# Prompt attention by pairs of heads: values and probabilities as two float32r parts in place of one float32 product

## Chip, cores and metric

One core of a Trainium2 chip. The metric is the device time of one execution in microseconds (us): a run's time is what counts, and the profile of one execution tells where it went. Engines are called as in the profile: PE (TensorE matmul), PEld (its weight load), DVE (VectorE), ACT (ScalarE), POOL (GpSimd), SP (SyncE, which issues the transfers).

## What is computed

Two decoder layers, for a prompt of 512 tokens and for 8 x 8 decode tokens. Each layer has a retention branch, an attention branch over the keys that an indexer selects, gates, and projections. The part around the change is the attention of the prompt, for 8 query heads that share 2 key/value heads (4 to 1) of 64 channels:

```
att = jnp.einsum('btkgd,btjkd->btkgj', qg, kg) * (ATT_HEAD_DIM ** -0.5)
att = jnp.where(valid[:, :, None, None, :], att, -jnp.inf)
p = jax.nn.softmax(att, axis=-1)
o = jnp.einsum('btkgj,btjkd->btkgd', p, vg)
```

The kernel doesn't gather: it scores all causal keys of a block of 128 queries, adds a large negative bias where the indexer left a key out, and takes the softmax over what is left.

## The kernel before

Everything is float32 in the reference. The kernel multiplies most of it as float32r (one pass through the array, fewer bits of the operands) in two parts: a matrix is split into a high part and the rest (`split`, `convert`), and products high x high, low x high and high x low are summed in PSUM. Activations are `xh`/`xl` (or `oh`/`ol`), weights `whi`/`wlo`; the big projections are `pm<-xh,whi`, `pm<-xl,whi`, `pm<-xh,wlo` with 288 or 256 columns. A few products are plain float32; the trace shows each of these as two records.

The tokens are five blocks: j = 0 to 3 are 128 prompt tokens each, j = 4 the 64 decode tokens. Per layer, in the order of `PLAN`: keys and values (`kx`), indexer (`iq`), retention values (`rv`), the attention gate (`az`), queries (`aq`, u = 0 and 1, four heads each), retention's q, k and gate for four heads (`rt0` to `rt3`), two of the eight gates of each branch (`gr`, `ga`), and from there on the merge (`wo`), which needs every branch to be done.

**Who sets the order.** All of this is written as generators (`head`, `kx`, `ret_p`, `ret_s`, `attend_s`, ...), the side streams, beside one main stream of projections. `Streams.go` emits instructions one by one: of all streams' next operations it takes the one that could start first by a model of the engines (`_duration`, `HOP`, `MARGIN`), and at equal starts the one of smaller `PRIO`. What is emitted is each engine's program order, and the engines run it in that order. All instructions are emitted in one line (293), so rows of the trace are told apart by tile names. The tiles `raw[0]`, `raw[1]` lie over the buffers `xh`, `xl` and carry those names.

For POOL the model charges the same for whatever operation (n is the number of elements of a partition):

```
    if eng == "POOL":
        return 0.3 + 0.165 * n
```

In before POOL only does powers of a few columns (`rsqrt`).

**Prompt attention** (`attend`, lines 925 to 944, and `head`, 898 to 921). For block j: 8 heads, at most `HEADS_IN_FLIGHT` = 3 at once. One head is a chain over four engines: scores (two matmuls into the one PSUM bank `tq`), the biased minimum on DVE (`CUSTOM_DVE`), exp with its sum on ACT, a reciprocal on DVE, the scaling on ACT, j + 1 transposes on PE into the one bank `ta`, a copy to SBUF on ACT (`t2k<-ta`), and j + 1 float32 products with 64 columns of values as stationary operand, into the one bank `oT`:

```
            for k in range(j + 1):
                yield PE.matmul(oT[kv * 64:(kv + 1) * 64, g * 128:(g + 1) * 128], av[:, k, kv * 64:(kv + 1) * 64],
                                PT[:, k * 128:(k + 1) * 128], start=k == 0, stop=k == j)
```

After all 8 heads of a block (`yield done`) DVE multiplies `oT` with the gate (`silz`), and the next block begins. The queries of a block, `qst[j, u]`, lie in one of 5 slots `QS`; probabilities and other intermediate tiles in 5 slots `T2` (`t2k`). The decode tokens have a stream of their own (`attend_s`, two groups g), which uses the same banks `tq`, `ta`, `oT`. So does the indexer with `tq`.

**The merge** waits for all side streams of the layer before it emits its splits `oh`/`ol` and the products with `wo` (line 1254):

```
                    for e in sides:
                        yield e
```

Of the kernel before, what the change touches and what calls it, by code (L numbers as in the profile page):

```python
# [11 lines left out]
FT = mybir.dt.float32  # L12
FR = mybir.dt.float32r
BF = mybir.dt.bfloat16
I32 = mybir.dt.int32
AF = mybir.ActivationFunctionType
OP = mybir.AluOpType
# [6 lines left out]
NS = 64  # L24
# [168 lines left out]


class Streams:
    """Emits the instructions of many sequential streams in the order in which a model of the engines could
    start them, so that each engine's program order follows what is ready."""

    HOP = {("DVE", "DVE"): 0.13, ("ACT", "ACT"): 0.13, ("POOL", "POOL"): 0.1, ("PE", "PE"): 0.0, ("SP", "SP"): 0.0,
           ("ACT", "PE"): 0.23, ("DVE", "PE"): 0.21, ("PE", "DVE"): 0.2, ("PE", "ACT"): 0.2, ("POOL", "DVE"): 0.07,  # L200
# [104 lines left out]
def tile_hybrid_decoder(ctx: ExitStack, tc: tile.TileContext, A, O):  # L305
    nc = tc.nc
    ctx.enter_context(tc.manual_schedule())
    K = Streams()
# [9 lines left out]
    def slots(pool, name, shape, dtype, n):  # L318
        return Slots([pool.tile(shape, dtype, name=f"{name}{i}") for i in range(n)])

    BANK = {n: slots(pb, n, [128, 512], FT, c) for n, c in BANKS.items()}
# [14 lines left out]
    def r3(ap, a):  # L336
        return ap.rearrange("p (a b) -> p a b", a=a)
# [51 lines left out]
    ready, paged = Event(), Event()  # L389
    second, third = Event(), Event()  # L390

    # ---- weights: one ordered sequence of units, each split into two float32r parts as it lands
    W = {}

    class Unit:
# [161 lines left out]
    def layer(l, xh, xl, kxb):  # L557
# [29 lines left out]
        at = atc.__enter__()  # L587
        raw = [xp.tile([128, KT * TX], FT, name="xh"), xp.tile([128, KT * T], FT, name="xl")]
        ro = 2 * (2 * T + 32)
        av = r3(raw[1][:, ro + 1152:ro + 1792], 5)  # L590
        iqss = raw[1][:, ro + 1792:ro + 2048].rearrange("p (b h t) -> p b h t", b=8, h=4)
        scs = [None] + [raw[1][:, ro + o:ro + o + (j + 2) * 128] for j, o in enumerate((0, 256, 640))]
        vr = r3(raw[0][:, 0:2560], 5)
# [14 lines left out]
        SM = slots(at, "sm", [128, 16], FT, 6)  # L608
        IQS = slots(at, "iqs", [128, 4, 128], FR, 2)
        QS = slots(at, "qs", [128, 4, 128], FR, NSLOT["qs"])  # L610
        T2 = slots(at, "t2k", [128, 512], FT, NSLOT["t2"])
        S4 = slots(at, "s4", [128, 8, 128], FT, NSLOT["s4"])
        TB = slots(at, "tb", [128, TH], FT, 2)
        SO = slots(at, "so", [128, 128], FT, 2)
# [63 lines left out]
        def kx(j, ps):  # L678
            yield ready
            yield e_r  # L680
            src, n, z = yield from pull(j, ps, 320)
            r = rcol[:n, j:j + 1]
            kt2 = yield Get(T2)
            kkt = kt2[:, :192]
            kk = r3(kkt[:n], 3)
            yield S.activation(kkt[:n], src[:, 0:192], AF.Copy, scale=r)
            yield S.activation(av[:n, j], src[:, 192:320], AF.Copy, scale=r)
            pulled(j, ps, z)
            kv = kk[:, 1:3]
            sqt = yield Get(SQ)  # L690
            sq = r3(sqt[:n, 0:128], 2)
            yield V.tensor_tensor(sq, kv, kv, OP.mult)
            yield from headnorm(kv, sq, n, 2)
            K.put(SQ, sqt)
            yield V.tensor_tensor(kv, kv, bc(gqk[:n, l, 1:2], [n, 2, 64]), OP.mult)
            yield from rope(kk, j, n, 3)
            rows = slice(j * 128, j * 128 + n)
            kdt = yield Get(KD)
            b = yield Get(BANK["ta"])
            if j < 4:  # L700
                kd = kdt[:, :384].rearrange("p (a b c) -> p a b c", a=3, b=2)
                yield S.activation(kd, bc(kk[:, :, None, :], [128, 3, 2, 64]), AF.Copy)
                for i in range(3):
                    yield PE.transpose(b[:, i * 128:(i + 1) * 128], flat(kd[:, i]), ident)
                K.put(KD, kdt)
                yield from split(kdh[:, :, rows], kdl[:, :, rows], r3(b[:, :384], 3))
            else:
                yield V.memset(kdt[:NS, 64:128], 0.0)
                yield V.tensor_copy(kdt[:NS, 0:64], kk[:, 0])
                yield PE.transpose(b[:, 0:NS], kdt[:NS, 0:128], ident[:NS, :NS])  # L710
                yield PE.transpose(b[:, NS:2 * NS], flat(kv), ident[:NS, :NS])
                K.put(KD, kdt)
                yield S.activation(flat(kts), b[:, :2 * NS], AF.Copy)
            K.put(BANK["ta"], b)
            K.set(e_kt[j])
            yield SP.dma_start(O["ik"][l, rows], kk[:, 0])
            yield SP.dma_start(O["k"][l, rows], flat(kv))
            yield SP.dma_start(O["v"][l, rows], av[:n, j])
            K.put(T2, kt2)
            K.set(e_k)  # L720

# [173 lines left out]
            yield S.activation(P, P, AF.Copy, scale=s)  # L895
            K.put(SM, sm)

        def head(j, u, g, kv, oT, done):
            L = max(256, (j + 1) * 128)
            bias = con("cb") if j == 0 else scs[j]  # L900
            q = qst[j, u][:, (g % 2) * 2 + kv]
            P = yield Get(T2)
            b = yield Get(BANK["tq"])
            ps = b[:, :L]
            yield PE.matmul(ps, q, kdh[:, 1 + kv, :L], start=True, stop=False)
            yield PE.matmul(ps, q, kdl[:, 1 + kv, :L], start=False, stop=True)
            yield from softmax(ps, bias, P[:, :L], b)
            PT = yield Get(T2)
            pT = yield Get(BANK["ta"])
            W_ = (j + 1) * 128  # L910
            for k in range(j + 1):
                yield PE.transpose(pT[:, k * 128:(k + 1) * 128], P[:, k * 128:(k + 1) * 128], ident)
            K.put(T2, P)
            yield S.activation(PT[:, :W_], pT[:, :W_], AF.Copy)
            K.put(BANK["ta"], pT)
            for k in range(j + 1):
                yield PE.matmul(oT[kv * 64:(kv + 1) * 64, g * 128:(g + 1) * 128], av[:, k, kv * 64:(kv + 1) * 64],
                                PT[:, k * 128:(k + 1) * 128], start=k == 0, stop=k == j)
            K.put(T2, PT)
            K.put(HD, None)  # L920
            K.set(done)

        HD = Slots([None] * HEADS_IN_FLIGHT)

        def attend():
            yield e_k
            for j in range(4):
                if j:
                    yield e_sc[j]
                oT = yield Get(BANK["oT"])  # L930
                done = Event(8)
                for u in range(2):
                    yield e_q[j, u]
                    for g in (2 * u, 2 * u + 1):
                        for kv in range(2):
                            yield Get(HD)
                            K.spawn(head(j, u, g, kv, oT, done), PRIO["attend"])
                yield done
                for u in range(2):
                    K.put(QS, qst[j, u])  # L940
                yield e_az
                z = silz[1][:, :, j * 128:(j + 1) * 128]
                yield V.tensor_tensor(z, r3(oT, 4), z, OP.mult)
                K.put(BANK["oT"], oT)

        def attend_s():
            yield paged
# [2 lines left out]
            for g in range(2):  # L950
# [11 lines left out]
                for kv in range(2):  # L962
# [20 lines left out]
                    yield S.activation(PT[:NS, 256:384], pT[:NS, 256:384], AF.Copy)  # L983
                    K.put(BANK["ta"], pT)
                    o = oS[:, kv * 64:(kv + 1) * 64]
                    yield PE.matmul(o, PT[:NS, 256:384], av[:NS, 4, hb], start=True, stop=True)
                    for b4 in range(4):
                        for i in range(2):
                            yield PE.matmul(o[b4 * 32:(b4 + 1) * 32],
# [473 lines left out]


PLAN = _plan("kx iq rv0 rv1 az0 az1 az2 az3 aq0 aq1 rt0 rt1 rt2 rt3")
HEADS_IN_FLIGHT = 3
PRIO = dict(convert=0, load=1, tables=6, indexer=7, indexer_s=3, attend=3, attend_s=5, ret_p=6, ret_s=4)
NSLOT = dict(s4=3, qs=5, t2=5, hi=3, lo=3)


def _prepare(x_prompt, x_sample, cache_k, cache_v, cache_idx_k, state_ret, page_table, p_prompt, p_sample,
# [79 lines left out]
```

## Time and profile before

| | us |
|---|---|
| median of 3 runs (1131.34 to 1132.42) | 1132.09 |
| span of the profiled execution | 1130.3 |
| median less span: what lies around the span | 1.8 |
| PE busy in the span | 1116.5 (99%) |
| DVE busy | 725.6 (64%) |
| ACT busy | 512.5 (45%) |
| POOL busy | 45.7 (4%) |

The profiled execution has no other time of its own in the result than its span; the 1.8 us around it are taken from the median. The profile's page gives the busy time of each engine, their shares in 40 slices of the span, the chain of work that ended last, and the costliest groups of instructions. A row of a group has the engine, the operation, the tile written and the tiles read, the shapes, the count, the busy time of all and the mean duration of one. Matmuls are pipelined: one lasts 0.28 us in the trace while the next starts after 0.12, so a matmul's cost to PE is read from the starts of two that follow each other.

### The profile page before, as it was taken

Reading aid. Unit: us, or ns where it says so; the run is one execution under the profiler, and the core shown is the slowest. Engines: PE = TensorE matmul, PEld = TensorE weight load, DVE = VectorE, ACT = ScalarE, POOL = GpSimd, SP = SyncE. Lnnn points to the kernel's source line nnn. Section 1 sums busy time; section 2 is a strip of 40 time slices with the busy share of each in tenths; the row PEclk is TensorE's granted clock in tenths of the full one; section 3 lists DMA queues with packets and bytes.
Section 4 is the critical chain, followed back from the end, with each engine's and each line's share of the span. In section 5 each row is a group of like instructions: output and inputs, shape, how many; then the busy total and the mean of one; then the engine's idle time right before and its main releaser. Section 6 shows DMA issues by size and latency. Waiting matters only on the chain.

```text
span 1130.3 us, 21562 instructions
## 1 busy us (share of the span) xinstructions
PE 1116.5 (99%) x8586; PEld 1058.9 (94%) x8586; DVE 725.6 (64%) x1883; ACT 512.5 (45%) x1084; POOL 45.7 (4%) x52
## 2 busy tenths in 40 slices
PE   8999999999999999999999999999999999999998
PEld 7899988888899999999999999888889999999998
DVE  6799988876464444543658999888654553544343
ACT  6643566647443232324546336656563422222331
POOL 0100200000000000000010012000000000000000
PEclk9999999999999999999999999999999999999999
DMA  6442221322122222523336112222212222234231
GB/s 196 139 133 76 76 75 52 102 78 78 59 75 75 93 76 92 172 92 109 100 118 181 59 57 94 74 79 80 73 60 78 75 78 91 75 130 144 93 113 48
DMA packets 43895, 105.92 MB, mean 94 GB/s; under 512 B 6418, under 2 KB 18578, under 8 KB 43794
## 3 DMA queue, kind: packets, MB, share of 16 engines
q1 hardware_dynamic: 43794, 104.55, 27.4%
q8 instruction: 67, 1.10, 0.4%
q14 instruction: 34, 0.28, 0.1%
HBM read 93.61 MB, written 10.91 MB: 92 GB/s over the span
## 4 chain that ended last, share of the span: by engine, by line
PE 91%; DVE 4%; DMA 2%; ACT 2%; issue 1%; SPq 0%; POOL 0%; DVEq 0%; ACTq 0%; POOLq 0%
PE pm L293 72%; PE oT L293 5%; PE tq L293 4%; PE acc L293 3%; PE tr L293 3%; PE ta L293 3%; DVE wlo L293 1%; DMA wst<-in_wb 1%; ACT whi L293 1%; DVE misc L293 1%; DMA x<-in_xT 1%; DVE silz L293 0%; DMA wst<-in_wq 0%; DVE qs L293 0%; DVE ol L293 0%
## 5 line engine op out<-in xcount | busy, mean ns | idle before, releaser
L293 PE MATMUL pm<-xl,whi 128*128 128x288 f32 x1536 | 458.7, 299 | 0.0
L293 PE MATMUL pm<-xh,wlo 128*128 128x288 f32 x1536 | 458.4, 298 | 0.0
L293 PE MATMUL pm<-xh,whi 128*128 128x288 f32 x1536 | 458.0, 298 | 0.4 <-DVE misc L293 0.4
L293 PEld LDWEIGHTS pm<-xl,whi 128*128 128x128 f32 x1536 | 290.1, 189 | 3.2 <-issue 2.4
L293 PEld LDWEIGHTS pm<-xh,whi 128*128 128x128 f32 x1536 | 290.2, 189 | 2.9 <-issue 1.6
L293 PEld LDWEIGHTS pm<-xh,wlo 128*128 128x128 f32 x1536 | 289.9, 189 | 1.8 <-issue 1.4
L293 ACT ACTIVATE whi<-wst 128x1024 fp32r<-128x1024 f32 (+4 forms) x148 | 150.5, 1019 | 280.5 <-PE pm L293 207.7
L293 DVE TENSOR_TENSOR wlo<-wst,whi 128x1024 fp32r<-128x1024 f32 (+4 forms) x148 | 173.0, 1171 | 88.8 <-ACT whi L293 88.5
L293 PE MATMUL pm<-whi,xh 128*128 128x256 f32 (+2 forms) x416 | 117.2, 288 | 0.7 <-ACT xl L293 0.7
L293 PE MATMUL pm<-wlo,xh 128*128 128x256 f32 (+2 forms) x416 | 117.0, 289 | 0.0
L293 PE MATMUL pm<-whi,xl 128*128 128x256 f32 (+2 forms) x320 | 91.0, 284 | 0.0
L293 DVE TENSOR_TENSOR misc<-pm,R 128x288 f32<-128x288 f32 x64 | 29.2, 457 | 90.1 <-PE pm L293 88.7
L293 ACT ACTIVATE t2k<-t2k,sm 128x256 f32<-128x256 f32 (+3 forms) x136 | 75.6, 581 | 22.6 <-DVE sm L293 19.4
L293 PEld LDWEIGHTS pm<-whi,xh 128*128 128x128 f32 x416 | 78.7, 189 | 2.5 <-issue 1.2
L293 PEld LDWEIGHTS pm<-wlo,xh 128*128 128x128 f32 x416 | 78.7, 189 | 1.6 <-issue 1.1
L293 PE MATMUL pm<-oh,whi 128*128 128x288 f32 x240 | 71.0, 296 | 0.0
L293 PE MATMUL pm<-oh,wlo 128*128 128x288 f32 x240 | 70.9, 296 | 0.0
L293 PE MATMUL pm<-ol,whi 128*128 128x288 f32 x240 | 70.9, 295 | 0.0
L293 PEld LDWEIGHTS pm<-whi,xl 128*128 128x128 f32 x320 | 60.5, 189 | 0.1
L293 ACT ACTIVATE misc<-misc 128x288 f32<-128x288 f32 x64 | 27.9, 436 | 60.5 <-DVE misc L293 60.5
L293 DVE MAX8 sm<-xl 128x8 f32<-128x384 f32 (+2 forms) x96 | 52.3, 548 | 0.3
L293 DVE SCALAR_TENSOR_TENSOR misc<-misc,pm 128x288 f32<-128x288 f32 x60 | 26.8, 451 | 39.3 <-PE pm L293 39.3
(231 smaller groups left out, 1654.3 us busy)
## 6 DMA issues: line engine op xcount, KB each, us to landing
wst<-in_wa SPq DMA_DIRECT2D x96, 512.0 KB, 3.5
wst<-in_wb SPq DMA_DIRECT2D x16, 512.0 KB, 4.1
wst<-in_wo SPq DMA_DIRECT2D x16, 512.0 KB, 3.4
s<-in_ckv SPq DMA_DIRECT2D x32, 128.0 KB, 2.4
s<-in_s SPq DMA_DIRECT2D x8, 512.0 KB, 4.3
out_rss<-s SPq DMA_DIRECT2D x8, 512.0 KB, 2.6
x<-in_xT SPq DMA_DIRECT2D x8, 288.0 KB, 4.5
misc<-in_xT SPq DMA_DIRECT2D x8, 288.0 KB, 3.6
```

Of the source, the lines that this page charges most:

```text
L293: op.fn(*op.a, **op.k)
```

## The change

For the prompt, the values get a second form: `vhl[:, k]` (128 keys x 256 columns, float32r) holds for each key/value head its 64 columns in a high and a low part, as [high 0 | low 0 | low 1 | high 1]. It is written in `kx` by two copies on ACT and two subtractions on DVE a block.

`head` becomes `score` (to the end of the softmax) and `pair`, which takes the two heads of one u and one kv together. Their transposes go side by side into `ta`, for two blocks of keys at a time; ACT copies them as float32r (`pth`, high part), DVE writes the rest (`ptl`), each with one buffer. Each block of keys then takes two products of 256 columns with the full 128 x 128 array: stationary [high | low] values, moving `pth`, then `ptl`. So rows 0 to 63 of the result have one of the parts of the values and rows 64 to 127 the other; a new stream `collect` adds the two halves (a copy on ACT, an addition on DVE, for each kv) and multiplies with the gate on POOL.

`attend` now has one bank `oT` and one `done` for each (j, u): it spawns two pairs, waits for both, then goes on to the next u. `PAIRS_IN_FLIGHT` is 2, `QS` has 4 slots, `T2` four own slots and one in `raw[1]`. Scores, softmax, the number of transposes, the decode attention and the retention stay.

```diff
+        vhl = at.tile([128, 4, 256], FR, name="vhl")
...
-        T2 = slots(at, "t2k", [128, 512], FT, NSLOT["t2"])
+        PTH = slots(at, "pth", [128, 512], FR, NSLOT["pt"])
+        PTL = slots(at, "ptl", [128, 512], FR, NSLOT["pt"])
+        T2 = slots(at, "t2k", [128, 512], FT, NSLOT["t2"] - 1)
+        T2.free.append(raw[1][:, ro + 1280:ro + 1792])
...
+            if j < 4:
+                for i, (h, o) in enumerate(((0, 64), (192, 128))):
+                    vh = vhl[:, j, h:h + 64]
+                    yield S.activation(vh, v[:, i * 64:(i + 1) * 64], AF.Copy)
+                    yield V.tensor_tensor(vhl[:, j, o:o + 64], v[:, i * 64:(i + 1) * 64], vh.bitcast(FT), OP.subtract)
...
+        def pair(j, u, kv, oT, first, done):
+            Ps, evs = [], []
+            for i in range(2):
+                P = yield Get(T2)
+                ev = Event()
+                K.spawn(then(score(j, qst[j, u][:, i * 2 + kv], kv, P), ev), PRIO["attend"])
+                Ps.append(P)
+                evs.append(ev)
+            o = oT[:, kv * 256:(kv + 1) * 256]
+            for k0 in range(0, j + 1, 2):
+                ks = range(k0, min(k0 + 2, j + 1))
+                w = len(ks) * 256
+                pT = yield Get(BANK["ta"])
+                for i in range(2):
+                    yield evs[i]
+                    for k in ks:
+                        yield PE.transpose(pT[:, (k - k0) * 256 + i * 128:(k - k0) * 256 + (i + 1) * 128],
+                                           Ps[i][:, k * 128:(k + 1) * 128], ident)
...
+                hi = yield Get(PTH)
+                lo = yield Get(PTL)
+                yield S.activation(hi[:, :w], pT[:, :w], AF.Copy)
+                yield V.tensor_tensor(lo[:, :w], pT[:, :w], hi[:, :w].bitcast(FT), OP.subtract)
+                K.put(BANK["ta"], pT)
+                for k in ks:
+                    for x in (hi, lo):
+                        yield PE.matmul(o, vhl[:, k, kv * 128:(kv + 1) * 128], x[:, (k - k0) * 256:(k - k0 + 1) * 256],
+                                        start=not first, stop=k == j and x is lo, skip_group_check=True)
...
+        def collect(j, u, oT, done):
+            yield done
+            t = yield Get(T2)
+            o = t[:, :256]
+            for kv in range(2):
+                mine, other = slice(kv * 64, kv * 64 + 64), slice(64 - kv * 64, 128 - kv * 64)
+                c = slice(kv * 256, (kv + 1) * 256)
+                yield S.activation(o[mine], oT[other, c], AF.Copy)
+                yield V.tensor_tensor(o[mine], oT[mine, c], o[mine], OP.add)
+            K.put(BANK["oT"], oT)
+            yield e_az
+            z = silz[1][:, 2 * u:2 * u + 2, j * 128:(j + 1) * 128]
+            yield G.tensor_tensor(z, r3(o, 2), z, OP.mult)
+            K.put(T2, t)
...
                 for u in range(2):
                     yield e_q[j, u]
-                    for g in (2 * u, 2 * u + 1):
-                        for kv in range(2):
-                            yield Get(HD)
-                            K.spawn(head(j, u, g, kv, oT, done), PRIO["attend"])
-                yield done
+                    oT = yield Get(BANK["oT"])
+                    done, first = Event(2), []
+                    for kv in range(2):
+                        yield Get(HD)
+                        K.spawn(pair(j, u, kv, oT, first, done), PRIO["attend"])
+                    last.append(Event())
+                    K.spawn(then(collect(j, u, oT, done), last[-1]), PRIO["attend"])
+                    yield done
                     K.put(QS, qst[j, u])
...
-HEADS_IN_FLIGHT = 3
+PAIRS_IN_FLIGHT = 2
...
-NSLOT = dict(s4=3, qs=5, t2=5, hi=3, lo=3)
+NSLOT = dict(s4=3, qs=4, t2=5, pt=1, hi=3, lo=3)
```

Three places show how the order moves. First PE in the last prompt block (j = 3) of layer 0, before. `tq` rows are scores, `ta` rows transposes of the probabilities, `oT` rows the products with the values, `pm` rows projections of the main stream:

```order
L293 MATMUL oT_73<-t2k_382,xl 64x128 x4
L293 MATMUL tq_71<-kdh,qs_378 128x512
L293 MATMUL tq_71<-kdl,qs_378 128x512
L293 MATMUL ta_72<-cst,t2k_384 128x128 x4
L293 MATMUL pm_68<-xl,whi_90 128x288
L293 MATMUL pm_68<-xh,wlo_93 128x288
L293 MATMUL pm_68<-xh,whi_90 128x288
```

Six more projections follow before the next head's `oT` row; after the layer's last `oT` row 169 more stand before the merge. The same block now (`tr` rows are the retention's):

```order
L293 MATMUL tq_71<-kdh,qs_381 128x512
L293 MATMUL tq_71<-kdl,qs_381 128x512
L293 MATMUL tr_74<-xl 128x128
L293 MATMUL ta_72<-cst,t2k_384 128x128 x2
L293 MATMUL tr_74<-cst,xl 128x128 x4
L293 MATMUL oT_73<-pth_382,vhl 128x256
L293 MATMUL oT_73<-ptl_383,vhl 128x256
```

No projection stands in it any more: of layer 0's PE order, the last 247 matmuls ahead of the merge (numbers 1944 to 2190 of the program) hold the decode attention's second group, the blocks (2,1), (3,0), (3,1) and the last retention pieces, and not one `pm` row; 134 projections in a row stand right ahead of them. The end of it, with the first row of the merge:

```order
L293 MATMUL oT_73<-pth_382,vhl 128x256
L293 MATMUL oT_73<-ptl_383,vhl 128x256
L293 MATMUL tr_74<-cst,xh 128x128 x4
L293 MATMUL pm_68<-oh_3775,whi_89 128x288
```

Where 169 projections stood between the last product with the values and the merge, now there is none. Layer 1 has the same stretch (numbers 5958 to 6204). Two shorter ones without projections stand earlier in each layer: 112 matmuls with the decode attention's first group and block (1,1) (1536 to 1647 in layer 0), and 34 with the end of block (1,0) (1356 to 1389). ACT at the start of block (3,0), now (`t2k,sm<-t2k,sm` is an exp with its sum, `t2k<-t2k,sm` the scaling of a head's probabilities):

```order
L293 ACTIVATE t2k_386,sm_375<-t2k_386,sm_375 128x512
L293 ACTIVATE t2k_384,sm_371<-t2k_384,sm_371 128x512
L293 ACTIVATE t2k_386<-t2k_386,sm_375 128x512
L293 ACTIVATE t2k_385,sm_373<-t2k_385,sm_373 128x512
L293 ACTIVATE t2k_384<-t2k_384,sm_371 128x512
L293 ACTIVATE t2k_387,sm_374<-t2k_387,sm_374 128x512
```

Each head's scaling stands behind the next head's exp.

## Rows read from the trace of the kernel before

**Rows 1.** The page: busy us and shares; PE's granted clock in 40 slices.
```profile
PE 1116.5 (99%) x8586; PEld 1058.9 (94%) x8586; DVE 725.6 (64%) x1883; ACT 512.5 (45%) x1084; POOL 45.7 (4%) x52
...
PEclk9999999999999999999999999999999999999999
```

**Rows 2.** Stretches: length, busy us of PE, PEld, DVE, ACT, POOL, PEclk, DMA.
```profile
0.00:28.00 28.00, 22.45 (x140) 21.73 (x140) 17.29 (x29) 18.33 (x35) 0.28 (x5) 1.00 0.61 198
...
268.00:297.00 29.00, 29.00 (x212) 25.44 (x210) 13.13 (x44) 17.48 (x37) 1.01 (x1) 1.00 0.19 68
297.00:326.00 29.00, 29.00 (x239) 27.60 (x239) 15.24 (x40) 12.30 (x26) 1.70 (x2) 1.00 0.21 76
```

**Rows 3.** The page: chain that ended last, by engine.
```profile
PE 91%; DVE 4%; DMA 2%; ACT 2%; issue 1%; SPq 0%; POOL 0%; DVEq 0%; ACTq 0%; POOLq 0%
```

**Rows 4.** Timeline of PE around one float32 product (start, duration, then the instruction).
```profile
126.24 0.28 PE L293 MATMUL pm<-whi,xh 128*128 128x256 f32 x1
126.36 0.28 PE L293 MATMUL pm<-whi,xl 128*128 128x256 f32 x1
126.57 0.43 PE L293 MATMUL oT<-t2k,xl 128*64 128x128 f32 x2
126.94 0.39 PE L293 MATMUL pm<-wlo,xh 128*128 128x256 f32 x1
```

**Rows 5.** Timeline of PE around the layer's last four float32 products; the merge's first row.
```profile
295.23 0.29 PE L293 MATMUL pm<-xl,whi 128*128 128x288 f32 x1
295.46 1.09 PE L293 MATMUL oT<-t2k,xl 128*64 128x128 f32 x8
296.47 0.33 PE L293 MATMUL tr<-cst,xl 128*128 128x128 f32 x1
...
325.51 0.30 PE L293 MATMUL pm<-oh,whi 128*128 128x288 f32 x1
```

**Rows 6.** Timeline, block 3: scores to DVE; exp, sum and scaling on ACT.
```profile
271.29 0.47 PE L293 MATMUL tq<-kdh,qs 128*128 128x512 f32 x1
271.60 0.39 PE L293 MATMUL tq<-kdl,qs 128*128 128x512 f32 x1
272.14 0.69 DVE L293 CUSTOM_DVE_ANT_0 t2k<-tq,xl 128x512 f32<-128x512 f32 x1 [1.31 <-PE tq L293]
...
284.43 0.71 ACT L293 ACTIVATE t2k<-t2k,sm 128x512 f32<-128x512 f32 x1
...
285.46 0.72 ACT L293 ACTIVATE t2k<-t2k,sm 128x512 f32<-128x512 f32 x1 [0.23 <-DVE sm L293]
```

**Rows 7.** Timeline, block 3: four transposes and the copy behind them.
```profile
286.05 0.66 PE L293 MATMUL ta<-cst,t2k 128*128 128x128 f32 x4
...
286.74 0.60 ACT L293 ACTIVATE t2k<-ta 128x512 f32<-128x512 f32 x1 [0.56 <-PE ta L293]
```

**Rows 8.** DVE and ACT groups by shape: PSUM reads and the merge's splits.
```profile
L293 DVE TENSOR_TENSOR silz<-oT,silz 128x512 f32<-128x512 f32 x8 | 5.5, 687 | 1.1 <-PE oT L293 1.0
...
L293 DVE TENSOR_TENSOR qs<-ta,qs 64x256 fp32r<-64x256 f32 x32 | 13.5, 422 | 3.0 <-ACT qs L293 2.1
...
L293 ACT ACTIVATE qs<-ta 64x256 fp32r<-64x256 f32 x32 | 12.0, 376 | 11.4 <-PE ta L293 6.0 <-DVE qs L293 5.0
...
L293 ACT ACTIVATE xh<-acc,gs 128x128 f32<-128x128 f32 x48 | 18.9, 453 | 5.1 <-DVE gs L293 5.1
```

**Rows 9.** POOL groups by shape.
```profile
L293 POOL TENSOR_TENSOR sm<-rsm,mh 128x4 f32<-128x4 f32 x16 | 17.3, 1081 | 186.4 <-DVE rsm L293 180.2 <-DVE sm L293 6.1
...
L293 POOL TENSOR_TENSOR sm<-rsm,mh 128x2 f32<-128x2 f32 x8 | 6.7, 842 | 5.8 <-DVE rsm L293 5.7
```

**Rows 10.** Timeline of PE: decode attention, one pass (products of the last, scores of the next).
```profile
197.16 0.43 PE L293 MATMUL oT<-xl,t2k 64*128 64x64 f32 x2
...
197.90 0.43 PE L293 MATMUL tq<-xl,qss 64*128 64x64 f32 x2
...
198.87 0.40 PE L293 MATMUL pm<-xh,whi 128*128 128x288 f32 x1
```

More of the change, by code (lines that the diff above doesn't have):

```diff
@@ L589, in layer @@
         ro = 2 * (2 * T + 32)
-        av = r3(raw[1][:, ro + 1152:ro + 1792], 5)
+        avs = raw[1][:, ro + 1152:ro + 1280]
+        vhl = at.tile([128, 4, 256], FR, name="vhl")
         iqss = raw[1][:, ro + 1792:ro + 2048].rearrange("p (b h t) -> p b h t", b=8, h=4)
@@ L685, in kx @@
             kk = r3(kkt[:n], 3)
+            v = kt2[:n, 192:320] if j < 4 else avs[:n]
             yield S.activation(kkt[:n], src[:, 0:192], AF.Copy, scale=r)
-            yield S.activation(av[:n, j], src[:, 192:320], AF.Copy, scale=r)
+            yield S.activation(v, src[:, 192:320], AF.Copy, scale=r)
             pulled(j, ps, z)
@@ L717, in kx @@
             yield SP.dma_start(O["k"][l, rows], flat(kv))
-            yield SP.dma_start(O["v"][l, rows], av[:n, j])
+            yield SP.dma_start(O["v"][l, rows], v)
+            if j < 4:
[3 more added lines that the diff above has]
+                    yield V.tensor_tensor(vhl[:, j, o:o + 64], v[:, i * 64:(i + 1) * 64], vh.bitcast(FT), OP.subtract)
             K.put(T2, kt2)
@@ L896, in softmax, with score @@
             K.put(SM, sm)
-        def head(j, u, g, kv, oT, done):
+        def score(j, q, kv, P):
             L = max(256, (j + 1) * 128)
             bias = con("cb") if j == 0 else scs[j]
-            q = qst[j, u][:, (g % 2) * 2 + kv]
-            P = yield Get(T2)
             b = yield Get(BANK["tq"])
@@ L907, in head @@
             yield from softmax(ps, bias, P[:, :L], b)
[L908 to L918, printed above, removed]
@@ L919, in head @@
-            K.put(T2, PT)
-            K.put(HD, None)
-            K.set(done)
-        HD = Slots([None] * HEADS_IN_FLIGHT)
+        def pair(j, u, kv, oT, first, done):
[16 more added lines that the diff above has]
+                                           Ps[i][:, k * 128:(k + 1) * 128], ident)
+                if ks[-1] == j:
+                    for P in Ps:
+                        K.put(T2, P)
+                    K.put(HD, None)
+                hi = yield Get(PTH)
[7 more added lines that the diff above has]
+                                        start=not first, stop=k == j and x is lo, skip_group_check=True)
+                        first.append(None)
+                K.put(PTH, hi)
+                K.put(PTL, lo)
+            K.set(done)
@@ new lines, in layer @@
+        HD = Slots([None] * PAIRS_IN_FLIGHT)
+        def collect(j, u, oT, done):
[12 more added lines that the diff above has]
+            K.put(T2, t)
@@ L925, in attend @@
         def attend():
             yield e_k
+            last = []
             for j in range(4):
@@ L929, in attend @@
                     yield e_sc[j]
-                oT = yield Get(BANK["oT"])
-                done = Event(8)
                 for u in range(2):
                     yield e_q[j, u]
-                    for g in (2 * u, 2 * u + 1):
-                        for kv in range(2):
-                            yield Get(HD)
-                            K.spawn(head(j, u, g, kv, oT, done), PRIO["attend"])
-                yield done
-                for u in range(2):
+                    oT = yield Get(BANK["oT"])
[6 more added lines that the diff above has]
+                    yield done
                     K.put(QS, qst[j, u])
[L941 to L944, printed above, removed]
+            for ev in last:
+                yield ev
         def attend_s():
@@ L985, in attend_s @@
                     o = oS[:, kv * 64:(kv + 1) * 64]
-                    yield PE.matmul(o, PT[:NS, 256:384], av[:NS, 4, hb], start=True, stop=True)
+                    yield PE.matmul(o, PT[:NS, 256:384], avs[:NS, hb], start=True, stop=True)
                     for b4 in range(4):
```

## The prediction

> **What bounds the kernel now.** The page's busy shares come first [rows 1]: PE is busy 99% of the span, DVE 64%, ACT 45%. The chain of work that ended last agrees: 91% of it is PE [rows 3]. In the stretches, the one with the last prompt block of layer 0 (268 to 297 us) and the one from there to the merge (297 to 326) have PE busy all 29.00 us each, with ACT at 17.48 and 12.30 and DVE at 13.13 and 15.24 [rows 2]. So attention costs nothing but its PE time: its chain over four engines hides behind projections, because these stand between its steps in PE's order. After the last product with the values, at 296.47, the merge's first row comes only at 325.51 [rows 5]: 29 us of gate projections are left as cover when attention is done. A change here is worth its PE time if the cover stays, and the length of its chain where it goes.
>
> **The change, part by part.**
>
> PE saves the float32 products. A 256-column float32r matmul takes 0.12 us from start to start (126.24 to 126.36). One float32 product ahead of another projection takes 126.36 + 0.12 to 126.94, so 0.46 us with its entry and exit [rows 4]; four take 295.23 + 0.13 to 296.47, so 1.11 [rows 5]. That is 0.22 more for each further one. A layer has 8 heads in each block: 8 x (0.46 + 0.68 + 0.89 + 1.11) = 25.1, both layers 50. Now there are 80 products a layer of 256 columns, 160 x 0.12 = 19. **PE: -31 us.** Scores and transposes stay equal in number.
>
> Beside it DVE gets 48 subtractions out of PSUM (nearest row: 128x512 at 0.69), 32 additions (64x256 at 0.42) and 16 small ones, and loses 8 gate products (0.69) [rows 8]: some 22 + 7 + 13 + 3 - 6 = 39 us over both layers. ACT gets 32 copies (0.38) and 16 small ones, about 14. Where projections cover them, they cost nothing, and both engines have the room [rows 1].
>
> POOL gets 16 multiplications of 256 columns. Before has no such row. Its powers take 0.84 us for 2 columns and 1.08 for 4 [rows 9]: 0.84 is the bound from below, and the slope of 0.12 a column would give 31 us from above. I take 1 us: a multiplication is one step for each element, as DVE's (0.69 for 512 columns, rows 8), a power is not. The Trainium skill, GPSIMD Engine Reference (3.1 Elementwise), has 4497 ns for a two-input addition of 2048 columns; an estimate from that page is 0.56 us for 256, and by it the sum would not move, since nobody on PE waits for these but at the merge.
>
> What moves is the order. The planner charges 0.3 + 0.165 x 256 = 42.5 us for each such multiplication, and with `yield done` for each (j, u) it drains attention eight times a layer. So it lets projections run out ahead of attention: the order shows 134 projections in a row, then 247 matmuls without one, then the merge. PE takes its instructions in this order, whatever POOL really needs, so in this stretch each chain is in the open. Its length, for one layer:
>
> - Decode attention, second group, two passes of 6.1: scores 0.97 (197.90 to 198.87 [rows 10]), a softmax of 2.2 with two group-norm copies (0.45 each [rows 8]) ahead of its scaling in ACT's order, transposes 0.35, their copies 0.65, products 0.74 (197.16 to 197.90). **12.3 us.**
> - Block (3,0). A score starts DVE after 0.85 and DVE needs 0.69 [rows 6], then the one bank `tq` is free: a score each 1.6, the fourth at 5.3 with the retention's rows between. From exp to the end of the scaling takes 1.75 (284.43 to 285.46, and 0.72 [rows 6]); but each scaling stands behind the next head's exp, so the last probabilities are ready at 9.6. The first pair's first round is done by then. Three more rounds go one by one through the banks `ta`, `pth`, `ptl`: 0.69 from transposes to copy and 0.60 [rows 7], a hop of 0.2, 0.69 on DVE, a hop of 0.2, so 2.4 each, and 0.5 for the last products. **17.3 us**; (3,1), with more of the retention between its rows, **18.1**; (2,1), with 384 columns and shorter second rounds, **14**.
> - To the merge: two copies of `collect`, four group-norm copies of 0.45 [rows 8], transposes, a product and the first split: **4.8**.
>
> Together 66.5 us. PE's own work in it: 44 products (5.3), 50 transposes at 0.10 (5.0), 12 score pairs at 0.55 (6.6), the decode passes (3.4) and 96 retention matmuls at between 0.10 (a transpose) and 0.25 (a float32 product), of which I take 0.15, as many have 32 columns (14): 34. So PE idles **32 us**. The stretch of 112 matmuls, counted so, lasts 12.3 + 10.4 with 15 of work: **8**; the one of 34: **1.5**. A layer idles 42, both 84.
>
> The sum: -31 + 84 = +53. The span of 1130.3 becomes 1183, and with the 1.8 us around it, which bring the span to the median of 1132.09, about **1185 us**. From below, the heads keep the pace that block 3 has now, 28.5 us for 8 heads (the stretch from 268 to 296.5): 57 us in place of 66.5, no idling in the shortest stretch, so 2 x 32 - 31 = +33, **1165**. From above, a tenth more on all chains: 2 x 51 - 31, **1203**.
>
> **The rivals.**
>
> *Covered after all (0.10).* PE's saving is certain and the idling is a sum of many small waits. ACT has some 43 us of work in the long stretch (24 exps and scalings at 0.52 to 0.72, copies of 0.38 and 0.60, 16 group-norm copies). Were ACT never idle, PE would idle only 43 - 34 = 9 us there, and the time be 1132 - 31 + 18 = **1119**, faster. It decides at 15.5 us of idling a layer. For it: the four heads of a (j, u) overlap. Against: one `tq`, one `ta`, one `pth` and one `ptl`, and nothing of the next u can begin; even with cover, ACT was busy only 17.48 of 29 us in block 3 [rows 2].
>
> *PE's clock falls (0.16).* In before the granted clock is 1.00 in every slice [rows 1], in the first 28 us too, with PE busy 22.45 [rows 2]; here PE would be busy for half of 66 us. The Trainium skill, TensorE: Matmul & The Clock Gate (Why this matters for your kernels), has the engine fall back to its lower level when there are idle gaps between bursts of matmuls, and warns of such loops; no row of before shows it. At 1.2 GHz PE's steps on the chain would take twice as long: a score pair, four rounds of transposes and products, about 4.4 us a block of 3, 17 a layer with the others. 1185 + 34 = **1219**, slower.
>
> *POOL multiplies as slowly as it powers (0.04).* At 31 us each, POOL's queue would still hold two or three at the merge, which waits for all: about 55 us a layer more, **1295**. Against: the reason above.
>
> **How the numbers follow.** The forecast as summed has 0.70: **1185 us**. The range reaches down past the pace of before to 1158, with a part of the covered case beyond it, and up past the fallen clock to 1224. A measurement tells about 0.2% (2.3 us) from no change. The covered case holds faster (0.06), the same (0.03) and slower (0.01); all others are slower: 0.06, 0.03, 0.91.
>
> **What would show it.** PE's busy share falls to about 93%, in slices that lie at the end of each attention: a stretch of some 60 us with PE half idle ahead of the first `pm<-oh` row, and idle time there put down to ACT `pth`, `t2k` and DVE `ptl`. The group `oT<-pth,vhl` has 80 and `oT<-ptl,vhl` 80, at 0.12 from start to start. POOL's new rows lie near 1 us. The stretches from the merge on take as long as before. It is wrong if `pm` rows follow each other without a gap up to the merge, if the clock shows less than 1.00, or if PE idles outside these stretches.

## The result, and the profile after

The changed kernel takes 1265.63 us (median of 4 runs, 1261.17 to 1270.19) beside 1132.26 of the kernel before: ratio 1.118 [1.117, 1.120], 133 us slower. Forecast were 1185 with a range of 1158 to 1224: the sign held, the size did not. The span of the profiled execution is 1264.5 us.

The page of the changed kernel, busy shares and PE's granted clock in 40 slices (before: [rows 1]):

```profile
PE 1169.7 (93%) x8426; PEld 1090.1 (86%) x8426; DVE 764.8 (60%) x1971; ACT 527.6 (42%) x1116; POOL 57.8 (5%) x68
...
PEclk9999799798678999999999997996986789999999
```

Two things are to be read here. PE's idle time is span less busy: 1264.5 - 1169.7 = 94.8 us, where before had 1130.3 - 1116.5 = 13.8. That is 81 more; 84 were forecast. But PE's busy time rose by 53 us, although 160 cheaper products replaced dearer ones: the second line shows one cause. The clock, 1.00 throughout before, falls in each layer's attention. Its mean over the core, with the span:

```profile
core 0: 1264.5 us, clock 0.928
```

The levels are 1.2 and 2.4 GHz, so a mean of 0.928 is 14.4% of the span, 182 us, at the lower one. The two long stretches without projections of each layer (length; busy us of PE, PEld, DVE, ACT, POOL; PEclk, DMA share, GB/s):

```profile
232.40:262.80 30.40, 25.04 (x171) 17.50 (x170) 11.54 (x43) 13.59 (x40) 1.42 (x2) 0.66 0.21 72
303.70:390.20 86.50, 63.71 (x337) 42.18 (x336) 38.48 (x127) 40.33 (x100) 6.31 (x8) 0.68 0.08 26
859.40:889.80 30.40, 25.07 (x172) 17.75 (x170) 11.64 (x43) 13.50 (x40) 1.42 (x2) 0.66 0.23 72
930.80:1014.60 83.80, 61.01 (x337) 40.20 (x336) 38.49 (x127) 40.32 (x100) 6.30 (x8) 0.73 0.08 27
```

They lie where the order put them and last 86.5 and 83.8 us where 66.5 were forecast, 30.4 where 22.7 (12.3 + 10.4) were, at a mean clock of about 0.7. Two rounds of one block show a part of what that means (PE timeline, block (3,0); four transposes each time, then the products):

```profile
356.54 0.60 PE L293 MATMUL ta<-cst,t2k 128*128 128x128 f32 x4
357.82 0.38 PE L293 MATMUL oT<-pth,vhl 128*128 128x256 f32 x1 [0.69 <-ACT pth L293]
358.55 1.11 PE L293 MATMUL ta<-cst,t2k 128*128 128x128 f32 x4 [0.34 <-DVE ptl L293]
...
362.30 1.06 PE L293 MATMUL ta<-cst,t2k 128*128 128x128 f32 x4
```

The first round takes 2.0 us (356.54 to 358.55; 2.4 were forecast). The second, with the transposes at 1.11 us in place of 0.60, takes 3.75. Not all of that is the clock. The same two rounds in experiment 9, where the clock is at 1.00:

```profile
338.08 0.60 PE L300 MATMUL ta<-cst,t2k 128*128 128x128 f32 x4
...
340.09 0.66 PE L300 MATMUL ta<-cst,t2k 128*128 128x128 f32 x4 [0.34 <-DVE ptl L300]
...
342.86 0.60 PE L300 MATMUL ta<-cst,t2k 128*128 128x128 f32 x4
```

They take 2.01 and 2.77. So 1.0 us of the second is the clock; the rest of the difference stands at full clock too, where the copy to `pth` waits for the products of the round before.

And PE waits in a place that the prediction had not looked at: the transposes of the queries (`ta<-cst,misc`), in the middle of projections (PE timeline, layer 0):

```profile
132.24 0.44 PE L293 MATMUL ta<-cst,misc 128*128 128x128 f32 x2 [0.61 <-DVE ptl L293]
...
136.69 0.69 PE L293 MATMUL ta<-cst,misc 128*128 128x128 f32 x2 [3.89 <-DVE qs L293]
138.11 0.58 PE L293 MATMUL pm<-whi,xh 128*128 128x256 f32 x1 [0.73 <-DVE misc L293]
138.49 0.41 PE L293 MATMUL pm<-wlo,xh 128*128 128x256 f32 x1
138.71 0.41 PE L293 MATMUL pm<-whi,xh 128*128 128x256 f32 x1
...
143.28 0.58 PE L293 MATMUL tq<-kdh,qs 128*128 128x256 f32 x1 [0.95 <-DVE qs L293]
...
145.86 0.47 PE L293 MATMUL ta<-cst,misc 64*128 64x64 f32 x2 [1.78 <-DVE qs L293]
```

The waits add up to 8.0 us, and after the one of 3.89 the clock is down: projections of 256 columns start 0.21 to 0.22 us apart, not 0.12 as in [rows 4]. Layer 1 has the same waits (3.79 for the longest).

What held: the products and the POOL multiplications came as forecast. Groups of POOL by shape, and of PE by tile (minimum/median/maximum ns):

```profile
L293 POOL TENSOR_TENSOR silz<-t2k,silz 128x256 f32<-128x256 f32 x13 | 10.5, 808 | 157.3 <-DVE t2k L293 157.3
...
L293 POOL TENSOR_TENSOR silz<-xl,silz 128x256 f32<-128x256 f32 x3 | 2.2, 726 | 19.2 <-DVE xl L293 19.2
```
```profile
L293 PE MATMUL oT<-pth,vhl x80: 277/364/581, 129.6 to 1009.4; 128*128 128x256 f32 x80
L293 PE MATMUL oT<-ptl,vhl x80: 277/362/582, 130.1 to 1009.6; 128*128 128x256 f32 x80
```

A multiplication takes 0.8 us; the planner charges 42.5.

### The profile page after: what moved, and what is told of

Its sections match the earlier page's. It is cut to its first block, busy times and chain, and to the rows that moved or that the text cites. A ratio compares the mean times of both kernels' runs of the same rounds, so it can differ in the third digit from the quotient of the medians.

```text
span 1264.5 us, 21455 instructions
## 1 busy us (share of the span) xinstructions
PE 1169.7 (93%) x8426; PEld 1090.1 (86%) x8426; DVE 764.8 (60%) x1971; ACT 527.6 (42%) x1116; POOL 57.8 (5%) x68
## 3 DMA queue, kind: packets, MB, share of 16 engines
q8 instruction: 66, 1.08, 0.4%
## 4 chain that ended last, share of the span: by engine, by line
PE 78%; DVE 13%; ACT 5%; DMA 2%; issue 1%; SPq 0%; POOL 0%; DVEq 0%; ACTq 0%; POOLq 0%
PE pm L293 61%; PE tq L293 4%; PE tr L293 4%; PE acc L293 4%; PE oT L293 3%; PE ta L293 3%; DVE xl L293 3%; DVE wlo L293 2%; DVE sm L293 2%; DVE misc L293 1%; DVE t2k L293 1%; ACT t2k L293 1%; DVE ptl L293 1%; ACT xh L293 1%; DMA wst<-in_wb 1%
## 5 line engine op out<-in xcount | busy, mean ns | idle before, releaser
L293 PE MATMUL pm<-whi,xh 128*128 128x256 f32 (+2 forms) x416 | 120.6, 295 | 2.2 <-DVE misc L293 1.5
L293 ACT ACTIVATE t2k<-t2k,sm 128x256 f32<-128x256 f32 (+3 forms) x108 | 62.3, 587 | 33.4 <-DVE sm L293 32.3
L293 PE MATMUL pm<-oh,whi 128*128 128x288 f32 x240 | 73.3, 305 | 0.2
```

The lines of the kernel that those rows point to most:

```text
L293: op.fn(*op.a, **op.k)
```

## The experiments

Three theories were to be told apart: the planner's charge makes the stretches (theory A); attention's own structure does, one bank each and the emptying after each (j, u) (B); the fallen clock is a cost of its own (C). All times below are medians, with the ratio to the kernel before.

**1. The gate's multiplication on DVE.** The changed kernel with

```
-            yield G.tensor_tensor(z, r3(o, 2), z, OP.mult)
+            yield V.tensor_tensor(z, r3(o, 2), z, OP.mult)
```

> The changed kernel with the gate's multiplication back on DVE (nothing left out). Theory A, the order: the planner's charge of 42.5 us for each of the 16 multiplications on POOL made it run out of projections; without it projections stand between the attention's steps again (no stretch of more than 47 matmuls without one, where there were 112 and 247), PE keeps nearly all of its saving of 31 us and the clock stays up: 1100 to 1118 us, granted clock over 0.99. Rival B, the drain: pairs that wait for each other eight times a layer through single banks are too long for any order: 1180 us or more, clock under 0.97, waits ahead of the merge as in the changed kernel.

Measured: 1165.49 us, 1.029 [1.027, 1.031]. A hundred of the 133 us go. Neither number was met: 1165 lies above A's 1118 and below B's 1180, so something besides the charge remains.

**2. The charge alone.** POOL still multiplies; the planner is told what the trace shows:

```
-        return 0.3 + 0.165 * n
+        return 0.8 if n == 256 else 0.3 + 0.165 * n
```

> The changed kernel with one number of the planner changed: 0.8 us for a POOL operation of 256 columns in place of 42.5 (the multiplication stays on POOL; nothing left out). Theory A: as with the multiplication on DVE, 1100 to 1118 us, and a little under it if DVE was short of time. Rival B: 1180 us or more. If POOL's multiplication itself holds something up (its queue, the powers behind it), this one is slower than the one on DVE by over 5 us.

Measured: 1160.29 us, 1.025 [1.023, 1.027]: -105 us by one number that changes no instruction, only their order. It is 5 us faster than experiment 1, so POOL's multiplication itself holds nothing up. What is left are 28 us over before, again above A's 1118. Attention still ends right at the merge (windows of layer 0, as above; the merge starts at 336.7):

```profile
302.00:320.00 18.00, 17.73 (x130) 16.45 (x129) 12.37 (x34) 10.62 (x23) 1.74 (x2) 1.00 0.19 68
320.00:337.00 17.00, 10.74 (x60) 8.55 (x58) 6.96 (x14) 8.63 (x18) 0.48 (x1) 0.80 0.18 58
```

**3. The charge without pairs.** The kernel before, with `oT` copied to SBUF and the gate's product done on POOL at the large charge:

```
+                t = yield Get(T2)
+                yield S.activation(t, oT, AF.Copy)
...
+                K.spawn(gate_z(j, t, last[j]), PRIO["attend"])
...
-                yield V.tensor_tensor(z, r3(oT, 4), z, OP.mult)
+                yield G.tensor_tensor(z, r3(t[:, u * 256:(u + 1) * 256], 2), z, OP.mult)
```

> The kernel before, heads and products as they were, with one part of the change: oT is copied to SBUF by ACT and the gate's multiplication goes to POOL, two of 256 columns a block, charged 42.5 us each (nothing left out). Theory A: the order alone does it: there is a stretch of 190 matmuls without a projection in each layer now, PE waits there, and the time is well over before: 1150 to 1190 us, clock under 1.00. Rival B: without pairs there is no drain, so 1132 us, 5 more or less.

Measured: 1233.28 us, 1.0895 [1.0877, 1.0913]. That is 101 us without any pair of heads, above A's 1190: the order has a stretch of 190 matmuls without a projection in each layer, in layer 0 from 202.6 to 278.9 us. The copy and POOL's part were not run here at the small charge, so this run alone doesn't separate them from it; experiment 2 does, in the changed kernel. There theory A is shown for some 105 of the 133 us.

**4. and 5. Extra matmuls to hold the clock.** The changed kernel with matmuls of 256 columns that compute nothing used: in 4 ahead of transposes and behind the decode scores, into the bank `ta` itself; in 5 only in the long stretch, into idle banks, but for the 20 of each decode pass, which go into `ta`. In both, the decode attention now takes `ta` ahead of its softmax, so there the edit is more than added matmuls.

> The changed kernel, its order unchanged, with 256 more matmuls of 256 columns a layer that nobody reads: 16 behind the scores of each decode pass, 4 ahead of each round of transposes of blocks 1, (2,1) and 3 (their result in the bank ta is overwritten by the transposes). They add up to 61 us of PE work where no wait covers them. Theory C: the lower clock, not the waits alone, makes the changed kernel as slow as it is: with the waits filled the clock stays up in the long stretches and the time falls in spite of the added work, to 1190 to 1235 us, mean clock over 0.96. If the waits bound the stretches whatever the clock, the time stays at 1266 or rises to 1290.

> The changed kernel with 392 further matmuls of 256 columns a layer, all in the long stretch ahead of the merge and into idle projection banks (they add work and compute nothing that is used): 20 behind the scores of the decode attention's second group, 5 behind each score and 8 behind the transposes of each round in the blocks (2,1), (3,0), (3,1). All other instructions keep their order, and no bank that attention waits for is held longer. At 0.12 us each they are 47 us a layer, put where PE waits. If the fallen clock lengthens the chains there (clock theory), the granted clock of the stretch rises to 0.95 or more and the stretch shrinks from 86.5 us to about 70: 1230 to 1242 us in all. If the chains are bound by waits for ACT and DVE alone and the clock only shows that PE waits (waits theory), the stretch stays at 86 us or grows: 1263 us or more.

Measured: 1261.38 us (1.1144 [1.1125, 1.1162]) and 1263.62 (1.1167 [1.1148, 1.1185]). The rows count 256 extra matmuls in 4 and 392 in 5, over both layers, half of what the expectations say: in 5 that is 196 a layer or 23.5 us. The long stretch of layer 0 in 5:

```profile
304.00:389.20 85.20, 70.31 (x533) 57.96 (x532) 38.85 (x127) 40.66 (x100) 6.31 (x8) 0.93 0.08 27
```

The clock rose from 0.68 to 0.93 and the length stayed. That looks like a verdict against C. But PE's busy time in the stretch rose by 6.6 us where 23.5 were added, so the old matmuls took some 17 less, and PE's idle time fell only from 22.8 to 14.9: at most 8 of the 23.5 us went into waits, and the rest used up what the higher clock gave. Both runs are inconclusive.

**6. Without the emptying.** The small charge of 2, and the next u may score before the bank `oT` of the last is free:

```
-                    oT = yield Get(BANK["oT"])
...
+                    K.spawn(grab(ref, have), PRIO["attend"])
...
-                    yield done
-                    K.put(QS, qst[j, u])
```

(`pair` waits for `have` ahead of its products; `collect` gives the slot back.)

> The kernel with the smaller charge for the POOL multiply, and one thing more: the first pair of the next u takes its scores before the bank oT of the last u is free (it waits for the bank only ahead of its products). If what is left of the loss, 28 us in that kernel, comes from attention being emptied eight times a layer (drain theory), attention ends earlier, projections stand beside its end again, the clock stays at 1.00 ahead of the merge, and the time is 1105 to 1135 us. If it comes from the one bank for transposes and the one buffer for each part (bank theory), little moves: 1150 to 1162 us.

Measured: 1144.24 us, 1.011 [1.009, 1.013]. -16: between the two, just under the bank theory's values. Ahead of the merge PE is now full (16.00 of 16.00 and 17.87 of 18.00 us busy from 297 to 331), so the emptying was that part. What remains is at the queries.

**7. The same with the large charge.**

> The changed kernel with its large charge for the POOL multiply, and the first pair of the next u allowed to take its scores before the bank oT is free. If the charge alone makes the loss (charge theory: each multiply still counts 42.5 us on the model's POOL, and the merge waits for them), the time stays within 10 us of the changed kernel's, 1255 to 1266. If emptying attention is what lets the charge reach PE's order (drain theory), the long stretch falls apart into shorter ones: 1205 to 1245.

Measured: 1318.79 us, 1.166 [1.164, 1.169]: both theories miss, the worst of all. Without the emptying, the end of block (3,1), the decode attention's second group and the retention's last pieces stand without a projection ahead of the merge. From the decode attention on, these are 60 us at a clock of 0.53:

```profile
354.20:414.60 60.40, 41.29 (x226) 26.64 (x225) 18.19 (x71) 15.28 (x44) 4.13 (x5) 0.53 0.08 29
```

So at the large charge the emptying was not what let it reach PE's order; the charge puts something in the open either way.

**8. Five query slots.** As 6, with `qs=5` and, for the space, `s4=2`.

> The kernel with the smaller charge and without the emptying between the u, and with five slots for queries as before (for which the decode states have two slots in place of three). If the lost slot delays the queries' projections (slot theory), the wait of 3.9 us ahead of the query transposes shrinks below 1.5 us, attention starts and ends earlier, and the time falls to 1115 to 1132 us. If it is the one bank for transposes and DVE's row of work that make that wait (bank theory), it stays near 3.9 us, and the time within 1136 to 1148.

Measured: 1213.31 us, 1.073 [1.070, 1.076]. It mixes two edits. The wait ahead of the query transposes stays (first row below), so the number of slots did not make it; and the third state slot, given up for it, was needed: the decode attention waits for a transfer (second row), and its second group with the retention behind it stands without projections from 328.3 to 363.1, at a clock of 0.57.

```profile
137.35 0.47 PE L293 MATMUL ta<-cst,misc 128*128 128x128 f32 x1 [3.79 <-DVE qs L293]
```
```profile
335.10 0.60 PE L293 MATMUL tq<-s,qss 64*32 64x256 f32 x1 [5.80 <-DMA s<-in_ckv]
```

**9. Extra matmuls in the gaps alone.** The lesson of 5: the order of the changed kernel, and extra matmuls only ahead of those rows that waited over 0.45 us in its trace, each gap filled to three quarters.

```
+            if op.eng == "PE":
+                n = WARM.get(self.npe, 0)
+                self.npe += 1
+                if n and self.warm:
+                    self.warm(n)
             op.fn(*op.a, **op.k)
```

> The changed kernel in its own order, with 382 further matmuls of 256 columns (added work that computes nothing used), put only where its trace shows PE idle for over 0.45 us during the attention of a layer: 55 such gaps of together 70.6 us, each filled to about three quarters at 0.12 us for one (23 ahead of the query transposes that waited 3.89 us, 31 ahead of the decode transposes that waited 5.09). So they take no time from any instruction as long as the clock is at 1.00. If the fallen clock was a cost of its own (clock theory), the granted clock rises from 0.93 to 0.97 or more and the time falls by 30 to 60 us of the at most 74 that 148 us of PE work at half speed can give back: 1205 to 1236 us. If the chains are as long at either level (waits theory), the clock rises and the time stays: 1255 us or more.

Measured: 1229.92 us, 1.088 [1.086, 1.091]: -36 us (30 to 39 by the two intervals), with 382 more matmuls to do. The clock:

```profile
core 0: 1225.4 us, clock 0.990
```

The query transposes still wait, but the projections behind them are at full speed, 0.12 us apart (PE timeline; line 604 is that of the extra matmuls):

```profile
132.12 2.92 PE L604 MATMUL tr<-vhl 128*128 128x256 f32 x23
136.18 0.44 PE L300 MATMUL ta<-cst,misc 128*128 128x128 f32 x2 [1.14 <-DVE qs L300]
...
137.82 0.28 PE L300 MATMUL pm<-wlo,xh 128*128 128x256 f32 x1
137.94 0.28 PE L300 MATMUL pm<-whi,xh 128*128 128x256 f32 x1
```

and the stretches are shorter by 5.6, 13.2, 4.6 and 8.9 us:

```profile
230.20:255.00 24.80, 21.03 (x196) 15.47 (x195) 11.35 (x44) 13.29 (x41) 1.42 (x2) 1.00 0.26 88
295.90:369.20 73.30, 59.65 (x444) 44.00 (x443) 38.13 (x127) 40.06 (x100) 6.33 (x8) 1.00 0.09 31
833.80:859.60 25.80, 22.08 (x195) 16.43 (x194) 11.58 (x44) 13.42 (x41) 1.42 (x2) 0.93 0.24 85
900.40:975.30 74.90, 61.49 (x447) 45.76 (x446) 38.23 (x127) 40.16 (x100) 6.32 (x8) 0.98 0.09 31
```

Theory C is shown: of the 133 us, some 36 come back when the clock is held up. They are not beside the 105 of theory A but mostly within them: the small charge takes the stretches away, and with them the low clock (0.976 as the mean of experiment 2).

**10. The same on experiment 6.** 131 extra matmuls in its 20 gaps.

> The kernel with the smaller charge and without the emptying between the u, its order kept, with 131 further matmuls that compute nothing used in its 20 gaps of PE over 0.45 us during attention (25.0 us of idle time). Its low clock is 27 us with 21 us of PE work in it. Clock theory: no low clock is left and the time falls by 6 to 10 us, to 1134 to 1138. Waits theory: 1142 us or more.

Measured: 1136.76 us, 1.0045 [1.0031, 1.0060]: -7.5, within C's numbers.

**11. The bank taken later.** What holds the queries? In the changed `pair` the bank `ta` is taken first, and then the stream waits for the softmax; the queries' transposes need the same bank. As 6, with

```
+                for ev in evs:
+                    yield ev
                 pT = yield Get(BANK["ta"])
                 for i in range(2):
-                    yield evs[i]
```

> The kernel with the smaller charge and without the emptying between the u, and a pair takes the bank ta only when the softmax of both its heads is done (as a head did before the change); so far it holds the bank from the start and the queries' transposes stand behind it. If this holding makes the waits of 3.9, 0.9 and 2.1 us ahead of the query transposes and what the clock loses behind them (bank theory: 8 us of waits and 7 of low clock a layer), these waits go and the time falls to 1115 to 1132 us, not above before. If DVE's row of work makes them (DVE theory), they only move to another place, and the time stays at 1138 to 1150.

Measured: 1129.44 us, 0.9968 [0.9956, 0.9980], no longer slower than before. Below, the stage of the queries (116 to 152 us) in 6, then in 11:

```profile
116.00:134.00 18.00, 15.55 (x124) 14.51 (x122) 17.17 (x60) 9.98 (x24) 2.06 (x2) 1.00 0.18 59
134.00:152.00 18.00, 11.28 (x47) 10.14 (x48) 15.54 (x49) 6.29 (x13) 4.68 (x5) 0.64 0.18 60
```
```profile
116.00:134.00 18.00, 17.92 (x144) 17.15 (x145) 17.54 (x63) 10.66 (x25) 5.00 (x5) 1.00 0.19 59
134.00:152.00 18.00, 16.00 (x119) 15.31 (x117) 16.02 (x47) 9.53 (x22) 1.88 (x2) 1.00 0.28 89
```

PE issues 263 matmuls in the stage in place of 171, at a clock of 1.00, with DVE as busy as it was: the held bank made these waits, not DVE's load.

**12. And the query slot given back after the scores**, when its last reader is issued, not after the products.

```
             yield PE.matmul(ps, q, kdl[:, 1 + kv, :L], start=False, stop=True)
+            K.set(used)
```

(a stream `release` waits for four of these and does `K.put(QS, qst[j, u])`.)

> As the last one, and the queries' slot is given back as soon as the four scores that read it are issued, not when the products are done. If the four slots hold the queries back (slot theory), some us less than the last kernel, 1108 to 1128; if not, the same within 3 us.

Measured: 1116.01 us, 0.986 [0.985, 0.987]: with the pairs and POOL's multiplication as the change has them, 16 us faster than before. With the bank out of the way, the slots did hold the queries back: 13 us. Taken in this order, the steps are 105 us for the charge, 16 for the emptying, 15 for the bank and 13 for the slot, 149 in all: the loss of 133 and the gain of 16. Its page:

```profile
PE 1088.9 (98%) x8426; PEld 1046.6 (94%) x8426; DVE 756.9 (68%) x1971; ACT 524.4 (47%) x1116; POOL 58.8 (5%) x68
...
PEclk9999999999999999999999999999999999999999
```

PE is busy 27.6 us less than in [rows 1]: the change's saving, with the clock at full. 16 of it reach the time.

## Why the prediction was right in sign and wrong in size

*PE saves 31 us.* Right: 27.6 in experiment 12, where the clock hides nothing of it.

*POOL takes 1 us for a multiplication.* Right: 0.81 and 0.73. The rival with 31 us fell.

*DVE gets 39 us and ACT 14.* Right: 39.2 and 15.1 by the two pages.

*The charge empties the projections ahead of attention, and PE idles 42 us a layer.* Right in place and cause (experiment 2). The total of idle time, 81 against 84, is right by luck. About 16 of it lie at the query transposes, outside every stretch that was counted. In the four stretches of the first table PE idles 56 us, where 2 x (32 + 8) = 80 were forecast: they last longer, but PE is also busy longer in them, in the long one 63.7 us where 34 of work were summed. A part of that is the clock; another is that a matmul that stands alone is busy for 0.38 us (357.82), while the sum charged the 0.12 of one in a row.

*The chains.* Too short, and so is the sum. With the clock held up (experiment 9, 0.93 to 1.00 in these stretches; the extra matmuls stand in waits, so at most these) the long stretch takes 73.3 and 74.9, not 66.5, the shorter 24.8 and 25.8, not 22.7: 15 + 5 = 20 us. The first piece missed most: decode's second group takes 15.3 us there (the first score of (2,1) comes at 311.2), where 12.3 were summed (the terms listed for a pass make 5.8, not 6.1), because ACT and DVE first convert a tile of weights ahead of its softmax; (3,1) takes 21.0 for 18.1. The changed kernel's chain of waits at that place:

```profile
303.71 1.07 ACT whi L293
...
304.80 1.22 DVE wlo L293
```

*The stage of the queries.* Not looked at: 16 us. The prediction followed `ta` only among the rounds of attention; that the change takes this bank before the softmax, and that the queries' transposes queue behind it, stood in the code.

*The clock.* This is the step that failed: "The forecast as summed has 0.70", with PE at 1.00, so that the lower clock stands in the sum at nothing; the fallen clock had 0.16. The rival happened, and so did two of the prediction's own signs of being wrong: a clock under 1.00 (0.928) and idle time outside the stretches. Its price was nearly right (34 forecast, 36 measured as the loss that filling gives back), its chance was not: the same sum that had PE half idle for 66 us spoke for it, and against it stood one stretch of before, 28 us at 1.00 with PE busy 22.45 [rows 2], far denser than half. Even the rival's 1219 lies 47 us under the result, since the chains and the queries come on top of it. The Trainium skill, TensorE: Matmul & The Clock Gate (Why this matters for your kernels), has the engine fall to the lower level when gaps stand between bursts of matmuls; this trace agrees (0.66 to 0.73 in the stretches).

Added up, as an estimate: +53 as forecast, +3 for the smaller saving, +20 for the chains, +16 for the queries, +36 for the clock make 128 of 133 us; 5 are not assigned. The pages divide the same loss in another way, without experiment 9: PE idles 81 us more than before, as many as forecast within 3, and is busy 53 us more where 31 less were forecast. The same matmuls are busy for 1169.7 us here and for 1088.9 in experiment 12: these 81 us are what the sum left out. Experiment 9 takes some 49 of them away (1166.3 us busy, less 382 x 0.12 for the extra matmuls); that the other 32 are matmuls that stand alone is not shown.

Mean clock is not a price. At 1.00 throughout, 7.2% of the changed span, 91 us, would have been "saved"; experiment 9 raised the mean to 0.990, 79 of these 91, and got 36 us. The rest of the low clock probably lay over time in which PE waited, or over steps that were not the last to be waited for; no run separates the two. The Trainium skill, the same page (HAM oscillation — how this bites in real kernels), reckons the penalty as throttled time times one half, which is these 91 us; the runs here show less than half of it.

What stays open: by which wait in the planner's model the charge takes the projections away was not looked at (in 3 the stretch lies in the middle of the layer, in the changed kernel at its end); why the large charge without the emptying (7) is worse than with it was not followed further; whether the kernel before would also gain from giving its slots back earlier was not run; and where the 12 us go by which experiment 12 falls short of its saving: PE idles 25.4 us there (span 1114.3 less 1088.9) against 13.8 before, in many short waits that were not taken apart.

## What to carry to other kernels

When a planner sets the order, check its cost for an operation against the trace before moving work to an idle engine: one wrong constant (42.5 us for 0.8) cost 105 us without changing an instruction. A shared bank or slot is to be taken when its first writer is ready and given back after its last reader; here that was worth 28 us (experiments 11 and 12), as much as the change's saving. When a forecast has PE half idle over tens of us, price the lower clock into the forecast itself, and test it with extra matmuls placed only where PE already waits.

## What the runs showed of the hardware that was not expected

In layer 0 a wait of 3.89 us between projections was followed by some 16 projections at half speed (0.21 us apart, 138.49 on). Extra work can make a kernel faster: 382 matmuls in the gaps gave 36 us, 131 gave 7.5; where they did not stand in gaps (4 and 5) they took back what they brought. POOL multiplies 256 columns (0.81 us) in less time than it raises 4 to a power (1.08, [rows 9]).
